# A two-group encoder layer on one core: where the weights' rounding rests and the scaled row maxima are computed

## The chip, the core and the metric

The kernel runs on one core of a Trainium2 chip. A core has a matrix engine (TensorE, in the profile PE, with its weight loads as PEld), and three engines for elementwise work: VectorE (DVE), ScalarE (ACT) and GpSimd (POOL). Each executes its own list of instructions in the order in which it stands and waits on the others by semaphores. SyncE (SP) issues the transfers (DMA) here. SBUF is the on-chip working memory, PSUM the accumulation memory into which TensorE writes. The metric is device time in microseconds (us) of one execution, as the median over runs.

## The reference

One layer is applied to two groups (prompt and sample) of 1024 tokens by 1024 channels, with the same weights:

```
h    = rms_norm(x, norm_g) * (1 + scale) + shift        # scale, shift, gate from silu(c) @ w_ada + b_ada
proj = h @ w_in                                         # 5376 columns
qa, ka, va, za, qb, kb, vb, zb, ga, gb = split(proj)
# branch A: 8 query heads, 2 key/value heads of 64, QK rms norm, axial rotary positions
oa = softmax(qa ka^T / 8) va * silu(za)
# branch B: 4 heads, two softmax maps of 64 each, 128-wide values
ob = rms_norm((softmax(q1 k1^T / 8) - lam * softmax(q2 k2^T / 8)) vb, subln_g) * (1 - lam_init) * silu(zb)
merged = sigmoid(ga) * (oa @ w_proj_a) + sigmoid(gb) * (ob @ w_proj_b)
y = x + gate * (merged @ w_out)
```

Everything is float32.

## The kernel before, in words

A float32 matrix is split in two for TensorE: a rounded part in a fast float32 format (F32R), and the rest, that is, the original minus the rounded part. A product is then three matmuls: rounded by rounded, and each rounded part by the other's rest. So every weight that is loaded passes ScalarE, which writes the rounded copy (line 179 in `split_w`, line 222 in `load_w_proj`), and a subtraction, which writes the rest (lines 181 and 223). A tile of weights (`w`) comes in four pieces, each staged in a buffer `st` by one transfer and split by one copy and one subtraction of 128x512 numbers. In `split_w` the subtraction goes to GpSimd, except that every second piece goes to VectorE while the flag `alone[0]` is set, which is the case outside the attention. In `load_w_proj` it always goes to GpSimd.

For each group the program runs through stages. The head makes keys, values and the first queries. Then come six phases of attention: phases 0 and 1 are the two halves of branch A's heads, phases 2 to 5 the heads of branch B. Beside each phase the program lays the projections that a later phase needs (`qa_gen`, `qkb_gen`, `vb_gen`, matmuls in line 514) and pieces of the gate projections (`z_gen`, line 703), so that TensorE has work while a softmax is computed elsewhere. Behind the attention come the gated outputs (`gated_gen`), the two branch projections with the merge (`merge_gen`, line 976) and the output projection (`out_gen`, line 1005).

One step of the attention, `scores`, treats 128 queries by 1024 keys. TensorE writes the scores into one of two score banks (`s`, lines 734 and 735). VectorE takes each row's negated maximum (line 736, the column `m`) and multiplies it by the row's inverse rms `rs` (line 737). ScalarE computes the exponentials with that product as bias (line 738) into a tile `p`, which frees the score bank. VectorE transposes `p` in blocks of 32 (line 771, `flip`), and in branch B combines two maps before that (line 770). Transfers (line 776) bring the blocks into place in a tile `q`. For branch A, ScalarE rounds the result (line 784, into `hi`) and VectorE subtracts (line 785), before the value matmuls (lines 796 and 797; branch B: line 836). Line 813 writes branch A's outputs `oo`. GpSimd also does the rotary positions of the projected rows (lines 546 to 556) and an inverse root (line 532) while the attention runs; their results are turned by TensorE two pieces of tokens later (`LAG`).

What sets the order: `weave` interleaves the generators of a phase by shares. Each stream has a length (for attention multiplied by `ATT_W`, for gate pieces from `Z_SHARE`) and a lead (`IN_A` for the projections, `Z_A` for the gate pieces). `fill` in the last phase runs the rest of the gate pieces and the first `16 - TAIL` pieces of branch A's merge, and `TAIL` pieces stay for the stretch behind the attention. The emitted work is then ordered on each engine by a planner that runs the program in advance, with attention steps at a higher priority. So a change of an instruction's engine changes the rows' order on all engines.

Of the kernel before, what the change touches and what calls it, by code (L numbers as in the profile page):

```python
# [12 lines left out]
F32 = mybir.dt.float32  # L13
F32R = mybir.dt.float32r
AF = mybir.ActivationFunctionType
ALU = mybir.AluOpType
# [18 lines left out]


Z_SHARE = (
    (7, 19, 5, 3, 3, 4),
    (9, 14, 7, 3, 2, 6),
)  # L40
Z_HEAD = (6, 6)
Z_HEAD_A = (-0.4, -0.45)
ATT_W = (
    (1.07, 0.837, 1.1, 0.95, 1.07, 1.52),
    (1.15, 1.354, 1.035, 1.15, 0.85, 1.069),
)
IN_A = (
    (0.1, 0.05, 0.2, 0.05, 0.15, 0.1),
    (0.1, -0.05, 0.45, 0.15, 0.15, 0.65),
)  # L50
Z_A = (
    (0.1, 0.0, 0.4, 0.0, 0.0, 0.0),
    (0.15, 0.05, 0.35, 0.15, -0.1, -0.1),
)
LAST_ATT, LAST_FILL = (44, 26)
GATED_A = -0.3
TAIL = 6
TAIL_A = 0.3
LAG = 2

# [11 lines left out]
def weave(*streams):  # L72

    live = [[g, n, 0, ahead] for g, n, ahead in streams if n > 0]
    while live:
        s = min(live, key=lambda s: s[2] / s[1] - s[3])
        if next(s[0], None) is not None:
            s[2] += 1
        else:
            live.remove(s)  # L80


def drain(*gens):
    for g in gens:
        if g is not None:
            for _ in g:
                pass
# [3 lines left out]
def kernel(ctx: ExitStack, tc: tile.TileContext, t: dict):  # L91
    nc = tc.nc
# [18 lines left out]
    def nm(s):  # L111
        uid[0] += 1
        return f"{s}_{uid[0]}"

    def sbank():
        return ps_s.tile([P, 1024], F32, tag="s", name=nm("s"))

    alone = [True]
# [57 lines left out]
    def split_w(w, q, st):  # L176
        wh = w[:, q * 2 : q * 2 + 2, 0, :]
        wl = w[:, q * 2 : q * 2 + 2, 1, :]
        nc.scalar.activation(wh, st, AF.Copy)  # L179
        e = nc.vector if alone[0] and q % 2 else nc.gpsimd  # L180
        e.tensor_tensor(out=wl, in0=st, in1=wh.bitcast(F32), op=ALU.subtract)  # L181

    def split_early(what):
        w, sts = what
        for q, st in enumerate(sts):
            split_w(w, q, st)

    def load_w(pieces, early=False):

        w = wpool.tile([P, NCH, 2, 256], F32R, tag="w", name=nm("w"))  # L190
        sts = []
        for q in range(4):
            if early:
                if q % 2 == 0:
                    room = halves2(ptile())
                st = room[q % 2].rearrange("p (c n) -> p c n", c=2)
            else:
                st = spool.tile([P, 2, 256], F32, tag="st", name=nm("st"))
            sts.append(st)
            off = 0  # L200
            for src in pieces(q):
                n = src.shape[1]
                dma(st[:, :, off : off + n], src.rearrange("(c p) n -> p c n", p=P))
                off += n
            assert off == 256
            if not early:
                split_w(w, q, st)
        return (w, sts) if early else w
# [6 lines left out]
    def load_w_proj(br, half):  # L215

        w = wpool.tile([P, 4, 2, 512], F32R, tag="w", name=nm("w"))
        mat = t["w_proj_b" if br else "w_proj_a"][0]
        for c in range(4):
            st = spool.tile([P, 512], F32, tag="st", name=nm("st"))  # L220
            dma(st, mat[c * P : (c + 1) * P, half * 512 : (half + 1) * 512])
            nc.scalar.activation(w[:, c, 0, :], st, AF.Copy)
            nc.gpsimd.tensor_tensor(out=w[:, c, 1, :], in0=st, in1=w[:, c, 0, :].bitcast(F32), op=ALU.subtract)
        return w


# [500 lines left out]
    def softmax_unit(q, rs, sw, k, pt, su):  # L727


        m = tiny.tile([P, 1], F32, tag="m", name=nm("m"))  # L730
        s = sbank()
        for n in range(2):
            sl = slice(n * 512, (n + 1) * 512)
            nc.tensor.matmul(s[:, sl], q, k[:, sl], start=True, stop=False)  # L734
            nc.tensor.matmul(s[:, sl], sw, k[:, sl], start=False, stop=True)  # L735
        nc.vector.tensor_reduce(out=m, in_=s, axis=AX.X, op=ALU.max, negate=True)  # L736
        nc.vector.tensor_tensor(out=m, in0=m, in1=rs, op=ALU.mult)  # L737
        nc.scalar.activation(  # L738
            pt.rearrange("p (j c a) -> p j c a", j=4, c=8), s.rearrange("p (c a j) -> p j c a", c=8, j=4),
            AF.Exp, scale=rs, bias=m, accum_out=su,  # L740
        )

    def scores(u, i):

        nm_ = len(u["q"])
        t, m = i // nm_, i % nm_
        qt = u["pr"] * 2 + t
        if "sw" not in u:
            u["sw"] = swapped(u)
        pt = ptile()  # L750
        su = u["su"][:, qt : qt + 1] if m == 0 else tiny.tile([P, 1], F32, tag="su", name=nm("su"))
        softmax_unit(u["q"][m][:, qt * P : (qt + 1) * P], u["rs"](qt, m), u["sw"][:, m, t * P : (t + 1) * P], u["k"][m], pt, su)
        if m == 0:
            u[t] = [pt]
        else:
            f = tiny.tile([P, 1], F32, tag="r", name=nm("r"))
            nc.vector.reciprocal(f, su)
            nc.gpsimd.tensor_scalar(
                out=f, in0=f, scalar1=u["su"][:, qt : qt + 1], scalar2=nlam, op0=ALU.mult, op1=ALU.mult
            )  # L760
            u[t] += [pt, f]
        return t if m == nm_ - 1 else None
# [190 lines left out]
    def merge_gen(st, br, oT, mT):  # L953

        for half in range(2):
            w = load_w_proj(br, half)
            for hf in range(2):
                if not br:
# [143 lines left out]
    for g in range(2):  # L1102
        st = states[g]
# [37 lines left out]
        def fill():  # L1141
# [3 lines left out]
            drain(first)  # L1145
            yield from islice(merge, 16 - TAIL)

# [3 lines left out]
        alone[0] = True  # L1151
        weave((merge, TAIL, 0.0), (then[1][0], 2, TAIL_A))
        weave((merge_gen(st, 1, oT, mT), 8, 0.0), (then[1][1], 4, 1.0))
# [58 lines left out]
```

## Time and profile before

| | us |
|---|---|
| median of 3 runs | 1973.39 (1972.16 to 1973.81) |
| span of the profiled execution, first to last instruction | 1971.9 |
| TensorE busy | 1901.8 |
| VectorE busy | 1353.0 |
| ScalarE busy | 1012.0 |
| GpSimd busy | 680.9 |

For the profiled execution only its span is shown. A row of a group of instructions gives the line, the engine, the operation, what it writes and reads, the shapes, the count (x), then the busy us, the mean ns of one, and the idle us of the engine ahead of them with what ended it ("<-"). A row of one line's instructions gives min/median/max in ns after the count. A row of waits gives the engine and line that waited, what it waited for, the us in total, the times and the longest. A row of a timeline gives start, length, engine, line and work. A row of a stretch gives its bounds and length, then PE, PEld, DVE, ACT and POOL busy with counts, the granted TensorE clock, the share of the DMA engines and GB/s. L179 is line 179 of the kernel. In the changed kernel, the lines from 180 on have the same numbers as before (only the rounded copy moves from line 179 to 180).

### The profile page before, as it was taken

To read this page: it belongs to the slowest core of one execution; us is meant where nothing else is said; L and a number is where in the kernel's file an instruction comes from. 1 tells how busy PE (TensorE), PEld (TensorE's weight loads), DVE (VectorE), ACT (ScalarE), POOL (GpSimd) and SP (SyncE) were. 2 spreads that over 40 slices of the span, in tenths; PEclk is the share of its full clock that TensorE was granted. 3 is DMA by queue.
4 is the path that set the end of the run, shared out by engine and by line. 5 is a ranking of instruction groups with operands and counts; after the bars stand their busy time and mean duration, and the time that the engine had idled before them with its cause. 6 is when DMAs were issued, how large, how long until landed. Compare 5 with 4: busy or idle time off the path is not lost. (4 is left out here: it accounts for less than half of the span.)

```text
span 1971.9 us, 30870 instructions
## 1 busy us (share of the span) xinstructions
PE 1901.8 (96%) x10466; PEld 1619.1 (82%) x10466; DVE 1353.0 (69%) x2165; ACT 1012.0 (51%) x1920; POOL 680.9 (35%) x958
## 2 busy tenths in 40 slices
PE   8999999999989999999999999999999999998999
PEld 3888888888878985778889788888888889776887
DVE  4658876786888577757465598768878766776641
ACT  4447655565655353464323576556666444447410
POOL 2363511442446251322235344114444426322210
PEclk9899999999999999999999999999999999999999
DMA  9125545556454345865641355555555334478431
GB/s 315 33 89 149 144 139 149 158 156 174 127 144 111 89 117 173 272 234 179 222 151 44 115 144 167 148 149 157 156 152 161 98 102 119 120 222 267 166 102 75
DMA packets 271614, 295.26 MB, mean 150 GB/s; under 512 B 37856, under 2 KB 220256, under 8 KB 271456
## 3 DMA queue, kind: packets, MB, share of 16 engines
q1 hardware_dynamic: 271456, 293.28, 50.1%
q8 instruction: 84, 1.38, 0.3%
q14 instruction: 74, 0.61, 0.1%
HBM read 133.72 MB, written 42.01 MB: 89 GB/s over the span
## 5 line engine op out<-in xcount | busy, mean ns | idle before, releaser
L703 PE MATMUL f<-u,w 128*128 128x512 f32 x2184 | 561.3, 395 | 3.0 <-ACT w L179 1.3
L514 PE MATMUL f<-w,u 128*128 128x256 f32 x3456 | 489.6, 286 | 5.2 <-ACT ev L709 2.7
L514 PEld LDWEIGHTS f<-w,u 128*128 128x128 f32 x3456 | 460.7, 192 | 26.8 <-ACT ev L709 3.7
L703 PEld LDWEIGHTS f<-u,w 128*128 128x128 f32 x2184 | 396.8, 189 | 78.1 <-ACT w L179 1.8
L181 POOL TENSOR_TENSOR w<-st,w 128x512 fp32r<-128x512 f32 x166 | 227.8, 1391 | 463.2 <-ACT w L179 412.9
L736 DVE TENSOR_REDUCE m<-s 128x1 f32<-128x1024 f32 x256 | 310.2, 1217 | 55.1 <-PE s L735 52.0
L771 DVE STREAM_TRANSPOSE p<-p 128x1024 f32<-128x1024 f32 x192 | 238.0, 1241 | 112.8 <-ACT p L738 110.2
L785 DVE TENSOR_TENSOR q<-q,hi 128x512 fp32r<-128x512 f32 x256 | 193.9, 774 | 47.9 <-ACT hi L784 46.4
L738 ACT ACTIVATE p<-s,m,rsB 128x1024 f32<-128x1024 f32 x128 | 154.0, 1204 | 135.0 <-DVE m L737 103.3
L738 ACT ACTIVATE p<-s,m,rsA 128x1024 f32<-128x1024 f32 x128 | 153.8, 1202 | 128.1 <-DMA q<-p 95.8
L735 PE MATMUL s<-u,sw 128*128 128x512 f32 x512 | 205.0, 401 | 0.0
L784 ACT ACTIVATE hi<-q 128x512 fp32r<-128x512 f32 x256 | 153.2, 624 | 78.2 <-DMA q<-p 50.2
L179 ACT ACTIVATE w<-st 128x512 fp32r<-128x512 f32 x196 | 114.2, 626 | 101.9 <-DMA st<-in_w_in_dram 46.6
L976 PE MATMUL f<-u,w 128*128 128x512 f32 x552 | 136.4, 400 | 11.3 <-ACT ev L709 4.1
L796 PE MATMUL a<-hi,u 128*128 128x256 f32 x512 | 132.0, 284 | 4.8 <-DVE oo L813 3.1
L976 PEld LDWEIGHTS f<-u,w 128*128 128x128 f32 x552 | 104.8, 192 | 35.3 <-DVE u L987 4.6
L836 PE MATMUL a<-q,u 128*128 128x256 f32 x512 | 125.9, 385 | 5.6 <-DMA q<-p 1.9
L797 PE MATMUL a<-q,u 128*128 128x256 f32 x512 | 129.8, 287 | 0.5 <-DVE q L785 0.4
L734 PE MATMUL s<-u 128*128 128x512 f32 x256 | 109.5, 428 | 7.9 <-ACT p L738 4.0
L734 PE MATMUL s<-u,u 128*128 128x512 f32 x256 | 103.3, 404 | 13.8 <-ACT p L738 9.0
L836 PEld LDWEIGHTS a<-q,u 128*128 128x128 f32 x512 | 95.9, 193 | 21.6 <-issue 2.9
L735 PEld LDWEIGHTS s<-u,sw 128*128 128x128 f32 x512 | 97.4, 190 | 15.5
(186 smaller groups left out, 2639.1 us busy)
## 6 DMA issues: line engine op xcount, KB each, us to landing
q<-p SPq DMA_DIRECT2D x768, 128.0 KB, 2.6
st<-in_w_in_dram SPq DMA_DIRECT2D x132, 256.0 KB, 3.0
zd<-ev SPq DMA_DIRECT2D x96, 256.0 KB, 2.2
sw<-u SPq DMA_DIRECT2D x256, 64.0 KB, 2.0
p<-zd SPq DMA_DIRECT2D x64, 256.0 KB, 3.8
u<-in_w_ada_dram SPq DMA_DIRECT2D x8, 1024.0 KB, 10.4
st<-in_w_in_dram SPq DMA_DIRECT2D x64, 128.0 KB, 2.7
st<-in_w_out_dram SPq DMA_DIRECT2D x32, 256.0 KB, 3.2
```

The costliest lines, as they stand in the source:

```text
L181: e.tensor_tensor(out=wl, in0=st, in1=wh.bitcast(F32), op=ALU.subtract)
L514: nc.tensor.matmul(ps, lt[c][:, sl], w[:, c, wi, :], start=(k == 0), stop=(k == 23))
L703: nc.tensor.matmul(ps, w[:, c, wi, e * P : (e + 1) * P], rt[c], start=(k == 0), stop=(k == 23),)
L734: nc.tensor.matmul(s[:, sl], q, k[:, sl], start=True, stop=False)
L735: nc.tensor.matmul(s[:, sl], sw, k[:, sl], start=False, stop=True)
L736: nc.vector.tensor_reduce(out=m, in_=s, axis=AX.X, op=ALU.max, negate=True)
L738: nc.scalar.activation(pt.rearrange("p (j c a) -> p j c a", j=4, c=8), s.rearrange("p (c a j) -> p j c a", c=8, j=4), AF.Exp, scale=rs, bi ...
L771: nc.vector.transpose(pt, pt)
L784: nc.scalar.activation(th, tl.bitcast(F32), AF.Copy)
L785: nc.vector.tensor_tensor(out=tl, in0=tl.bitcast(F32), in1=th.bitcast(F32), op=ALU.subtract)
L836: nc.tensor.matmul(acc, u["v"][:, k], pT[:, k], start=(k == 0), stop=(k == 7))
L976: nc.tensor.matmul(ps, w[:, c, wi, d * P : (d + 1) * P], o[:, oi, :], start=(k == 0), stop=(k == 11))
```

## The change

Three things. The subtraction that makes a weight's rest is always put on VectorE, in `split_w` and in `load_w_proj`. The product of row maximum and inverse rms in `softmax_unit` becomes an activation of ScalarE (a copy with a scale) in place of a multiplication on VectorE. And numbers that share out the phases are set anew: in `Z_SHARE`, `ATT_W`, `IN_A`, `Z_A`, and `TAIL` from 6 to 4.

```diff
 Z_SHARE = (
-    (7, 19, 5, 3, 3, 4),
-    (9, 14, 7, 3, 2, 6),
+    (6, 20, 5, 3, 3, 4),
+    (9, 14, 7, 2, 2, 7),
 )
 ATT_W = (
-    (1.07, 0.837, 1.1, 0.95, 1.07, 1.52),
+    (1.129, 0.837, 1.289, 0.95, 1.039, 1.314),
...
-TAIL = 6
+TAIL = 4
...
         nc.scalar.activation(wh, st, AF.Copy)
-        e = nc.vector if alone[0] and q % 2 else nc.gpsimd
-        e.tensor_tensor(out=wl, in0=st, in1=wh.bitcast(F32), op=ALU.subtract)
+        nc.vector.tensor_tensor(out=wl, in0=st, in1=wh.bitcast(F32), op=ALU.subtract)
...
             nc.scalar.activation(w[:, c, 0, :], st, AF.Copy)
-            nc.gpsimd.tensor_tensor(out=w[:, c, 1, :], in0=st, in1=w[:, c, 0, :].bitcast(F32), op=ALU.subtract)
+            nc.vector.tensor_tensor(out=w[:, c, 1, :], in0=st, in1=w[:, c, 0, :].bitcast(F32), op=ALU.subtract)
...
         nc.vector.tensor_reduce(out=m, in_=s, axis=AX.X, op=ALU.max, negate=True)
-        nc.vector.tensor_tensor(out=m, in0=m, in1=rs, op=ALU.mult)
+        nc.scalar.activation(m, m, AF.Copy, scale=rs)
```

Counted over the program, 168 subtractions of `split_w` and 32 of `load_w_proj` go from GpSimd to VectorE (32 of `split_w` were there already), 256 products go from VectorE to ScalarE, and ScalarE's list has 41 loads of an activation table where it had 38. All other instructions are the same in number.

In the first phase of the first group, VectorE's rows before the change (numbers behind names count the buffers; `m` is the row maximum, `s` the scores, `q` and `hi` the probabilities and their rounded part, `u` projected keys and queries):

```order
L736 TENSOR_REDUCE m_2466<-s_2467 128x1
L785 TENSOR_TENSOR q_2225<-q_2225,hi_2349 128x2x8x32
L785 TENSOR_TENSOR q_2225<-q_2225,hi_2362 128x2x8x32
L736 TENSOR_REDUCE m_2516<-s_2517 128x1
L570 TENSOR_TENSOR u_1456<-f_2733,u_1456 64x2x128
L737 TENSOR_TENSOR m_2466<-m_2466,rsA_120 128x1
L737 TENSOR_TENSOR m_2516<-m_2516,rsA_120 128x1
```

Two reductions stand together there, and the product of the first waits behind two subtractions, the second reduction and a key's subtraction. VectorE's rows of the changed kernel at the corresponding place, where the weights `w_3045` arrive (`st` is the staged piece, `ss` and `row` belong to a projected row's norm):

```order
L736 TENSOR_REDUCE m_2436<-s_2437 128x1
L181 TENSOR_TENSOR w_3045<-st_3046,w_3045 128x2x256
L181 TENSOR_TENSOR w_3045<-st_3050,w_3045 128x2x256
L181 TENSOR_TENSOR w_3045<-st_3054,w_3045 128x2x256
L570 TENSOR_TENSOR u_1456<-f_2759,u_1456 64x2x128
L530 TENSOR_REDUCE ss_2750<-row_2747 128x4
L736 TENSOR_REDUCE m_2478<-s_2479 128x1
```

The products are gone from this list, and three rests of one weight tile stand between two reductions. ScalarE's rows of the changed kernel at the same place:

```order
L180 ACTIVATE w_3045<-st_3046 128x2x256
L180 ACTIVATE w_3045<-st_3050 128x2x256
L180 ACTIVATE w_3045<-st_3054 128x2x256
L569 ACTIVATE u_1456<-f_2759 64x2x128
L528 ACTIVATE row_2747<-row_2747 128x256
L709 ACTIVATE ev_2817<-f_2612 128x512
L784 ACTIVATE hi_2261<-q_2084 128x512
L784 ACTIVATE hi_2321<-q_2180 128x512
L737 ACTIVATE m_2436<-m_2436,rsA_120 128x1
L784 ACTIVATE hi_2343<-q_2180 128x512
L738 ACTIVATE p_2435,suA_117<-s_2437,m_2436,rsA_120 128x1024
```

The rounded copies of the three pieces stand together, and the product L737 now stands in ScalarE's list behind other copies, with one more copy between it and its exponential.

More of the change, by code (lines that the diff above doesn't have):

```diff
@@ L43 @@
 ATT_W = (
-    (1.07, 0.837, 1.1, 0.95, 1.07, 1.52),
-    (1.15, 1.354, 1.035, 1.15, 0.85, 1.069),
+    (1.129, 0.837, 1.289, 0.95, 1.039, 1.314),
+    (1.255, 1.354, 1.035, 1.175, 0.85, 1.069),
 )
 IN_A = (
-    (0.1, 0.05, 0.2, 0.05, 0.15, 0.1),
-    (0.1, -0.05, 0.45, 0.15, 0.15, 0.65),
+    (0.1, 0.25, 0.2, 0.05, 0.15, 0.1),
+    (0.1, -0.05, 0.45, 0.25, 0.15, 0.65),
 )
@@ L52 @@
     (0.1, 0.0, 0.4, 0.0, 0.0, 0.0),
-    (0.15, 0.05, 0.35, 0.15, -0.1, -0.1),
+    (0.2, 0.05, 0.35, 0.35, -0.1, 0.1),
 )
-LAST_ATT, LAST_FILL = (44, 26)
+LAST_ATT = 44
+LAST_FILL = 26
 GATED_A = -0.3
-TAIL = 6
+TAIL = 4
 TAIL_A = 0.3
```

## Prediction

> **What bounds the kernel now.** I read the page's busy times first, then the list of who waited for whom, then busy times by stretch, then the lines that the change touches.
>
> ```profile
> span 1971.9 us, 30870 instructions
> PE 1901.8 (96%) x10466; PEld 1619.1 (82%) x10466; DVE 1353.0 (69%) x2165; ACT 1012.0 (51%) x1920; POOL 680.9 (35%) x958
> 1867.52 5.44 PE f L976 x24
> ```
>
> The last row (from the chain that ended last) shows PE at its undisturbed pace: 24 matmuls of 512 columns in 5.44 us, 227 ns each. The change leaves PE's work alone, so only PE's idle time can be won: 1971.9 - 1901.8 = 70.1 us, the head and the tail included. The profiled span lies 1.5 us under the median of the runs, 1973.39 us; I make the sum against the span and add the 1.5 us at the end. A move of under 0.2% (4 us) is what a measurement of this kernel cannot tell from none.
>
> Which part of the 70 us could the change reach? The list of PE's waits (time, times, longest):
>
> ```profile
> PE s L734 <- ACT p L738: 13.0, 15, 1.6
> PE s L734 <- DMA q<-p: 6.1, 4, 3.6
> PE f L976 <- ACT ev L709: 4.1, 1, 4.1
> PE f L976 <- DVE u L987: 3.9, 3, 2.6
> PE a L796 <- DVE oo L813: 3.1, 4, 1.2
> PE f L976 <- DVE row L946: 3.0, 2, 2.5
> PE a L836 <- DMA q<-p: 1.9, 3, 0.8
> PE f L703 <- POOL w L181: 0.3, 1, 0.3
> ```
>
> The largest wait is that of the next score matmuls (L734) for an exponential (L738), which frees one of two score banks: 13.0 us in 15 waits, 0.87 us each. The transfers of the transposed probabilities (6.1 + 1.9 us) and the values' output (3.1 us) hang on the same chain. That makes 24.1 us behind the softmax. For the weights' rests on POOL the PE waited 0.3 us in all.
>
> **The softmax step.** What the chain waits for, by line:
>
> ```profile
> ACT p L738 <- DVE m L737: 124.5, 59, 5.9
> L737 DVE TENSOR_TENSOR m<-m,rsA x128: 111/159/1251, 144.5 to 1467.2; 128x1 f32<-128x1 f32 x128
> L737 DVE TENSOR_TENSOR m<-m,rsA 128x1 f32<-128x1 f32 x128 | 30.1, 238 | 2.1
> L737 DVE TENSOR_TENSOR m<-m,rsB 128x1 f32<-128x1 f32 x128 | 25.9, 209 | 1.7
> L736 DVE TENSOR_REDUCE m<-s 128x1 f32<-128x1024 f32 x256 | 310.2, 1217 | 55.1 <-PE s L735 52.0
> L738 ACT ACTIVATION_READ_ACCUMULATOR p<-s,m,rsB 128x1 f32 x128 | 24.4, 191 | 0.0
> L569 ACT ACTIVATE u<-s x26: 257/274/381, 80.3 to 1093.3; 64x128 fp32r<-64x128 f32 x14, 64x256 fp32r<-64x256 f32 x12
> ```
>
> ScalarE waited 59 times for the small product L737. Its own 159 ns (the middle figure: median) is not the trouble; its place in VectorE's queue is. Where the old order puts a second reduction and two subtractions ahead of it, as in the rows of the order above, that is 1.217 + 2 x 0.686 us. The change takes 30.1 + 25.9 = 56.0 us off VectorE and gives ScalarE 256 instructions that the trace does not show. Nearest rows: 191 ns for a 128x1 read of the accumulator below, 274 ns for a small activation above. Near the lower one, since it is a 128x1, I take 0.20: 256 x 0.20 = 51 us (49 to 70) on an engine busy 1012 us. The Trainium skill's page "ScalarE: Activation LUTs" (What ACT_TABLE_LOAD costs) puts an activation with one 128x1 pointer operand at about 280 ns, by which it would be 72 us; no run yet shows which.
>
> Per softmax the chain trades 0.16 us plus its place in VectorE's queue for 0.20 us plus its place in ScalarE's. The second can also be behind other work: in the order above, one subtraction input (L784) stands between product and exponential. Bounds on the gain: at best all 24.1 us, at worst a loss as large. I take a third, -8: a wait of 0.87 us ends when a reduction of 1.217 us no longer stands in between, but only where such a pair exists and ScalarE is free.
>
> **The weights' rests.** 168 instructions of split_w and 32 of load_w_proj move from POOL to VectorE.
>
> ```profile
> L181 POOL TENSOR_TENSOR w<-st,w x166: 1259/1296/2247, 47.1 to 1926.7; 128x512 fp32r<-128x512 f32 x166
> L181 DVE TENSOR_TENSOR w<-st,w x30: 672/693/1785, 47.6 to 1931.0; 128x512 fp32r<-128x512 f32 x30
> L181 DVE TENSOR_TENSOR w<-st,w 128x512 fp32r<-128x512 f32 x30 | 31.5, 1051 | 27.4 <-ACT w L179 27.3
> L785 DVE TENSOR_TENSOR q<-q,hi x256: 631/686/1836, 159.5 to 1511.5; 128x512 fp32r<-128x512 f32 x128
> L785 DVE TENSOR_TENSOR q<-q,hi 128x512 fp32r<-128x512 f32 x256 | 193.9, 774 | 47.9 <-ACT hi L784 46.4
> 480.88 2.99 POOL L181 TENSOR_TENSOR w<-st,w 128x512 fp32r<-128x512 f32 x2
> 481.13 3.29 DVE L785 TENSOR_TENSOR q<-q,hi 128x512 fp32r<-128x512 f32 x2 [1.32 <-ACT hi L784]
> ```
>
> Cost on VectorE at the median: 200 x 0.693 = 139 us. Against it stands a relief. The last two rows are one moment: two rests run on POOL, and two subtractions beside them take 3.29 us where the median makes 1.37. So a rest on POOL stretches a two-input subtraction of VectorE by up to its own length. Over the kernel: L785 has 193.9 us against 256 x 0.686 = 175.6 at the median, 18 us too much; L181 itself 31.5 against 30 x 0.693 = 20.8, 11 us. Also L737's mean of 238 against 159, already counted in the 56. VectorE's balance: 139 - 56 - 29 = +54 us, 1353 to about 1407 us, 71% of the span. POOL loses the whole of its 228 + 44 us in these groups.
>
> ```profile
> L181 POOL TENSOR_TENSOR w<-st,w 128x512 fp32r<-128x512 f32 x166 | 227.8, 1391 | 463.2 <-ACT w L179 412.9 <-DMA od<-oo 28.4 <-DVE q L1010 18.2
> L223 POOL TENSOR_TENSOR w<-st,w 128x512 fp32r<-128x512 f32 x32 | 44.0, 1395 | 106.9 <-ACT w L222 104.7 <-DMA tab<-rA 2.2
> 150.00:770.00 620.00, 604.28 (x3544) 526.91 (x3543) 461.59 (x712) 350.82 (x681) 234.10 (x360) 0.99 0.50 139
> 1110.00:1775.00 665.00, 644.08 (x3720) 562.38 (x3719) 506.59 (x766) 375.71 (x724) 247.35 (x377) 0.99 0.52 144
> ```
>
> What hid the rests before is that POOL could sit and wait for the weight's copy on ScalarE (412.9 us) with little behind it. On VectorE the wait stands in front of reductions. The 30 rests already there waited 27.3 us, 0.91 us each. The last two rows are the two attention stretches (columns after the length: PE, PE loads, VectorE, ScalarE, POOL): PE idle 15.7 + 20.9 = 36.6 us of 1285, VectorE idle 1285 - 968.2 = 316.8. An idle us of VectorE thus went with at most 36.6 / 316.8 = 0.115 us of PE's. Bounds for the added waits: 0, if the copies are early; 168 x 0.91 = 153 us on VectorE and 17.7 on PE, if all are as late as the present ones. The planned order puts three copies ahead on ScalarE with a reduction in front of the three rests, so I take a sixth of the upper end, +3. The relief of 29 us by the same ratio is worth -3.3; the 139 us of added work fill idle time of VectorE, which the two stretches have 317 us of.
>
> The Trainium skill's page "SBUF — State Buffer" (SBUF: two separate sides) says of GpSimd and a VectorE operation with two SBUF inputs that whichever starts first holds the shared port pair and the other "fully blocks". The 3.29 us agree for VectorE as the loser. Where the rule speaks against the change: it makes 200 more holders that block POOL's rotary work, which stays there.
>
> ```profile
> L546 POOL TENSOR_TENSOR rc<-row,cosB x64: 317/323/1400, 354.8 to 1697.0; 128x64 f32<-128x64 f32 x64
> ```
>
> In rows: 323 ns at the median and 1400 at most, so a block costs POOL about 1.1 us. If one in four of the 200 met such an operation, 55 us of waits would be added to an engine that loses 272 us of work: nothing for PE, whose rotated rows are needed two pieces later (LAG).
>
> **Pieces set anew.** These move matmuls between stages and take none away. Shares of each phase shift the score matmuls among projections by a few positions; bounds are the waits of one phase either way, some 10 us (24.1 over two groups, less than half each); I take 0. TAIL 6 to 4 brings two branch-A merges of 12 matmuls forward, 2 x 12 x 0.227 = 5.4 us per group. They are cover taken from the stretch after the attention, where PE waited 4.1 + 3.9 + 3.0 us, and given to its last scores. Between -5 and +11; I take 0, since what is cover lost behind is cover won ahead. ScalarE's order holds 41 table loads instead of 38; a load is 1283 ns (median of L738's), so 3.8 us there, by the ratio 0.4 us on PE: +0.4.
>
> ```profile
> L738 ACT ACT_TABLE_LOAD  x9: 1283/1283/1283, 144.0 to 1791.5; - x9
> ```
>
> **Sum.** -8 + 3 - 3.3 + 0.4 = -7.9, so a span of 1964.0 and a time of 1965.5 us.
>
> **Rivals.** (1) Rests late on VectorE. They arrive with their weights, and while VectorE stands at one, reductions behind it let the score banks stay full. At the present mean wait of 0.91 us PE loses 17.7, against the relief of 3.3 and nothing won in the softmax: +14, 1987 us. For it: 27.3 us in front of 30 rests. Against it: those are in the stages without attention, where weights come one after another. It decides once the mean wait is over (8 + 3.3) / (168 x 0.115) = 0.58 us. (2) ScalarE's queue takes the chain's wait over: a product planned early stops the three copies L784 behind it until its reduction is done. For it: L784 feeds the value matmuls and ScalarE already waited 124.5 us at this spot. Against it: the same wait stood there before, one instruction later. If it doubles, 124.5 us more of ScalarE's idle time, of which PE's share was at most 36.6 / (1285 - 726.5) = 0.066, cost 8.2; with nothing won in the softmax, the rests' +3 and the relief of 3.3 that is +8, 1981 us. It decides once that wait passes some 245 us. (3) Nothing moves: PE has 96% and its waits are spread over many causes; what the softmax releases is met by the next wait. 1973 us. (4) More is won: the whole 24.1 us goes but for 4, with evener spacing of the scores: -20, 1953 us. It needs ScalarE always free.
>
> **Chances.** Forecast 0.50 (own range 1956 to 1969); (4) 0.12; (3) 0.14; (1) 0.14; (2) 0.10. So faster 0.62, within 0.2% 0.14, slower 0.24. The range 1950 to 1987 takes in (2) to (4) and reaches to the price of (1); what is left out is the half of (1) that comes dearer and of (4) that comes cheaper, with the unpriced tail of the pieces, about 0.2.
>
> **What will show it.** Right: the wait of L738 for L737 gone and its successor (ScalarE's L737 for the reduction) under 124.5 us; L785 near 0.69 us on average instead of 774 ns; PE's waits for L738 and the transfers at some 14 us. Wrong: VectorE's L181 waiting more than 0.58 us each on ScalarE's copy; ScalarE's L737 above 0.3 us; waits of L976 in the merges above 11 us; PE idle for more than 36.6 us in the two attention stretches.

## The result and the profile after

The changed kernel takes 1959.89 us (median of 4 runs, 1956.9 to 1963.3) against 1973.6 us before. The ratio is 0.9936, with a 95% interval from 0.9920 to 0.9952. The forecast was 1965.5 us in a range from 1950 to 1987 us: the sign is as forecast and the time lies in the range. How it came about was otherwise than forecast.

The busy times of the profiled execution after, whose time was 1959.98 us:

```profile
span 1958.3 us, 30869 instructions
PE 1896.0 (97%) x10466; PEld 1618.1 (83%) x10466; DVE 1373.1 (70%) x2109; ACT 1081.4 (55%) x2179; POOL 408.2 (21%) x758
```

PE idles 62.3 us instead of 70.1, and its busy time is 5.8 us shorter for the same 10466 matmuls. So of the 13.6 us by which the span is shorter, 7.8 are idle time and 5.8 are busy time. PE's waits after, the rows that the text speaks of:

```profile
PE s L734 <- ACT p L738: 13.2, 14, 3.5
PE f L976 <- ACT ev L709: 5.0, 1, 5.0
PE a L797 <- DVE q L785: 4.2, 3, 1.9
PE f L858 <- ACT at L851: 4.1, 1, 4.1
PE a L796 <- DVE oo L813: 4.0, 6, 1.6
PE f L514 <- ACT ev L709: 2.3, 1, 2.3
PE a L796 <- DMA q<-p: 1.4, 1, 1.4
PE f L514 <- DVE w L181: 1.1, 2, 0.6
PE f L976 <- DVE u L987: 0.6, 1, 0.6
```

The wait for the exponentials, on which the forecast's largest term rested, is unchanged: 13.2 us, before 13.0. The waits for the transposed probabilities fell from 6.1 and 1.9 us to 1.4, and the merges' waits on VectorE (L987, L946) from 6.9 to 0.6. Others grew: the value matmuls' wait for the subtraction (L797) from 0.4 to 4.2 us, and the wait at L858, not in the list before, to 4.1. The idle time that was won is a sum of small waits. In the two attention stretches PE now idles 12.6 + 17.2 = 29.8 us, before 36.6:

```profile
150.00:770.00 620.00, 607.37 (x3549) 528.58 (x3547) 475.64 (x667) 385.17 (x804) 153.04 (x301) 0.99 0.51 142
1110.00:1775.00 665.00, 647.81 (x3739) 566.71 (x3738) 518.97 (x730) 413.58 (x859) 154.97 (x307) 0.99 0.54 150
```

The 5.8 us of busy time are spread over many lines (L703 has the most, 2.0 us), and no run here tells what shortened it. By line, the instructions that the change touches:

```profile
L737 ACT ACTIVATE m<-m,rsA x128: 278/294/297, 141.1 to 1461.1; 128x1 f32<-128x1 f32 x128
ACT m L737 <- DVE m L736: 195.7, 145, 5.4
L181 DVE TENSOR_TENSOR w<-st,w x196: 645/684/1529, 47.3 to 1915.6; 128x512 fp32r<-128x512 f32 x196
DVE w L181 <- ACT w L180: 33.3, 31, 2.5
L785 DVE TENSOR_TENSOR q<-q,hi 128x512 fp32r<-128x512 f32 x256 | 172.8, 691 | 40.9 <-ACT hi L784 39.7
```

The product takes 0.294 us on ScalarE. The rests wait 33.3 us on ScalarE's copies, 0.17 us each over the 196 shown. VectorE's subtractions L785 are down from 774 ns on average to 691, close to the 686 that were their median before. Where the time went between the groups is seen from the output projection's line, first of the kernel before, then of the changed one (first and last start stand behind the durations):

```profile
L1005 PE MATMUL f<-u,w x456: 388/389/389, 932.7 to 1967.8; 128*128 128x512 f32 x152
```

```profile
L1005 PE MATMUL f<-u,w x456: 388/389/390, 925.9 to 1954.0; 128*128 128x512 f32 x152
```

The first group's output begins 6.8 us earlier, and from there to the last output matmul 1028.1 us pass instead of 1035.1. Both groups won about 7 us.

### The profile page after: what moved, and what is told of

Read it like the earlier page. It is cut to its first block, busy times and chain, and to the rows that moved or that the text cites. A ratio compares the mean times of both kernels' runs of the same rounds, so it can differ in the third digit from the quotient of the medians.

```text
span 1958.3 us, 30869 instructions
## 1 busy us (share of the span) xinstructions
PE 1896.0 (97%) x10466; PEld 1618.1 (83%) x10466; DVE 1373.1 (70%) x2109; ACT 1081.4 (55%) x2179; POOL 408.2 (21%) x758
## 4 chain that ended last, share of the span: by engine, by line
PE 69%; DVE 10%; DMA 8%; ACT 5%; issue 4%; SPq 3%; POOL 1%; ACTq 0%; DVEq 0%; POOLq 0%
PE f L703 16%; PE f L514 16%; PE f L976 5%; PE f L1005 5%; PE s L734 4%; PE a L836 4%; PE s L735 4%; PE s L1005 4%; DVE m L736 3%; DMA q<-p 3%; PE s L976 2%; PE a L797 2%; PE a L796 2%; SPq L776 2%; DVE p L771 2%
## 5 line engine op out<-in xcount | busy, mean ns | idle before, releaser
L703 PE MATMUL f<-u,w 128*128 128x512 f32 x2184 | 559.4, 395 | 0.4 <-ACT ev L709 0.3
L703 PEld LDWEIGHTS f<-u,w 128*128 128x128 f32 x2184 | 398.4, 189 | 76.9 <-ACT ev L709 0.9
L735 PE MATMUL s<-u,sw 128*128 128x512 f32 x512 | 204.9, 400 | 0.0
L785 DVE TENSOR_TENSOR q<-q,hi 128x512 fp32r<-128x512 f32 x256 | 172.8, 691 | 40.9 <-ACT hi L784 39.7
L784 ACT ACTIVATE hi<-q 128x512 fp32r<-128x512 f32 x256 | 153.7, 624 | 67.3 <-DMA q<-p 43.6
L738 ACT ACTIVATE p<-s,m,rsA 128x1024 f32<-128x1024 f32 x128 | 153.7, 1201 | 63.7 <-DMA q<-p 57.9
L738 ACT ACTIVATE p<-s,m,rsB 128x1024 f32<-128x1024 f32 x128 | 154.1, 1204 | 5.1 <-DVE p L770 1.0
L181 DVE TENSOR_TENSOR w<-st,w 128x512 fp32r<-128x512 f32 x196 | 132.5, 707 | 33.2 <-ACT w L180 32.1
L797 PE MATMUL a<-q,u 128*128 128x256 f32 x512 | 129.9, 287 | 4.2 <-DVE q L785 4.2
L836 PE MATMUL a<-q,u 128*128 128x256 f32 x512 | 125.2, 381 | 0.5 <-DMA st<-in_w_in_dram 0.4
L657 POOL TENSOR_TENSOR row<-row,gB 128x96 f32<-128x96 f32 x64 | 31.0, 484 | 452.3 <-ACT row L528 452.2
L734 PE MATMUL s<-u 128*128 128x512 f32 x256 | 109.7, 428 | 8.5 <-ACT p L738 8.4
L734 PE MATMUL s<-u,u 128*128 128x512 f32 x256 | 102.8, 402 | 7.6 <-ACT p L738 4.9
L735 PEld LDWEIGHTS s<-u,sw 128*128 128x128 f32 x512 | 97.6, 191 | 15.0
```

The costliest lines, as they stand in the source:

```text
L703: nc.tensor.matmul(ps, w[:, c, wi, e * P : (e + 1) * P], rt[c], start=(k == 0), stop=(k == 23),)
L738: nc.scalar.activation(pt.rearrange("p (j c a) -> p j c a", j=4, c=8), s.rearrange("p (c a j) -> p j c a", c=8, j=4), AF.Exp, scale=rs, bi ...
L785: nc.vector.tensor_tensor(out=tl, in0=tl.bitcast(F32), in1=th.bitcast(F32), op=ALU.subtract)
L836: nc.tensor.matmul(acc, u["v"][:, k], pT[:, k], start=(k == 0), stop=(k == 7))
```

## The experiments

The runs set three theories against each other. The softmax theory is the prediction's: the product wins by leaving VectorE's queue. The blocking theory says that the rests win by leaving GpSimd, where they held VectorE up. The numbers theory says that the new sharing of the phases wins. All times are medians; the kernel before ran beside each group of runs, at 1973.5 to 1974.5 us.

### One part at a time

The weights' rests alone:

```diff
-        e = nc.vector if alone[0] and q % 2 else nc.gpsimd
-        e.tensor_tensor(out=wl, in0=st, in1=wh.bitcast(F32), op=ALU.subtract)
+        nc.vector.tensor_tensor(out=wl, in0=st, in1=wh.bitcast(F32), op=ALU.subtract)
...
-            nc.gpsimd.tensor_tensor(out=w[:, c, 1, :], in0=st, in1=w[:, c, 0, :].bitcast(F32), op=ALU.subtract)
+            nc.vector.tensor_tensor(out=w[:, c, 1, :], in0=st, in1=w[:, c, 0, :].bitcast(F32), op=ALU.subtract)
```

> All weights' rests on VectorE, the product still on VectorE, the old numbers. Softmax theory (the prediction's: the gain comes from taking the product out of VectorE's queue): no change or a small loss, 1972 to 1978 us, L785 at about 0.69 us on average. Blocking theory (GpSimd's rests held VectorE up): most of the 13.7 us is here, 1960 to 1966 us. Numbers theory (the gain is the new sharing of the phases): within 4 us of 1973.6.

Measured: 1995.5 us, ratio 1.0098 (1.0080 to 1.0117), slower. VectorE was relieved as the blocking theory says, and it did not help. In this kernel lines stand one lower, so L784 is the subtraction that is L785 before; its row, the rests' wait, and the granted clock:

```profile
L784 DVE TENSOR_TENSOR q<-q,hi 128x512 fp32r<-128x512 f32 x256 | 173.2, 693 | 27.7 <-ACT hi L783 26.2 <-DMA zd<-ev 0.5
DVE w L180 <- ACT w L179: 36.2, 29, 3.5
core 0: 1993.7 us, clock 0.980
```

The rests wait 36.2 us in all, about as long as in the changed kernel (33.3), so the slowdown is not that VectorE stands at them. PE waits longer elsewhere, at the value matmuls of branch B (L835 here): 18.1 us in the four rows that name a transfer, against 3.2 at the same place (L836) before. The clock is 0.980 of full speed, in the kernel before 0.990; over the spans the missing shares are 39.9 us here and 19.7 us before. The blocking theory had set 1960 to 1966 us, and falls here.

The product alone:

```diff
-        nc.vector.tensor_tensor(out=m, in0=m, in1=rs, op=ALU.mult)
+        nc.scalar.activation(m, m, AF.Copy, scale=rs)
```

> The product of maximum and inverse rms on ScalarE alone, rests and numbers as before. Softmax theory: 1962 to 1968 us, PE's wait for L738 below 13 us. Blocking theory: within 4 us of 1973.6, L785 still near 0.77 us on average. Numbers theory: within 4 us of 1973.6.

Measured: 1980.77 us, ratio 1.0034 (1.0022 to 1.0046), slower, and outside what any of the theories had set. PE's longest wait and the clock:

```profile
PE s L734 <- ACT p L738: 21.3, 18, 3.7
core 0: 1977.7 us, clock 0.984
```

The wait for exponentials grew to 21.3 us. The softmax theory, as the prediction put it, falls: the product's move alone does not shorten that wait.

Both edits of engines, with the old numbers:

> Rests on VectorE and product on ScalarE, old numbers. Softmax theory and blocking theory: 1959 to 1966 us, nearly all of the gain, the numbers being worth little. Numbers theory: 1970 us or more.

Measured: 1978.4 us, ratio 1.0019 (1.0007 to 1.0032), some 4 us slower, which is the size that the forecast counts as no move. The numbers alone, with the engines as before:

> Only the new numbers, rests and product on the engines of before. Softmax and blocking theories: 1970 to 1980 us, no gain. Numbers theory: 1958 to 1966 us.

Measured: 1977.93 us, ratio 1.0008 (0.9997 to 1.0019), no difference shown. So no part wins by itself, and both engine edits together do not either; with the numbers they win 13.7 us. This left all three theories wrong as stated. A fourth came up, the fit theory: that the numbers fit the one order which the planner makes of this very program.

### One part left out

The changed kernel with the product back on VectorE (the reverse of the edit above):

> The changed kernel with the product back on VectorE; rests on VectorE and the new numbers stay. Softmax theory: loses most of the gain, 1968 to 1975 us. Blocking theory: keeps it, 1958 to 1964 us. Fit theory (the gain is that the new numbers suit the one order which the planner makes of this very program; any change of it loses them): 1968 us or more, and more in the half-speed time of the matrix engine's clock or in PE's waits of many small kinds.

Measured: 1991.73 us, ratio 1.0094 (1.0068 to 1.0120): all of the gain is lost and more. The changed kernel with the rests back on GpSimd:

> The changed kernel with the weights' rests back on GpSimd; product on ScalarE and the new numbers stay. Softmax theory: keeps the gain, 1958 to 1964 us. Blocking theory: loses it, 1968 to 1978 us, with VectorE's subtractions L785 back at some 0.76 us on average instead of 0.69. Fit theory: 1968 us or more.

Measured: 1959.79 us, ratio 0.9932 (0.9909 to 0.9956): the whole gain, without the rests' move. Against this stand the blocking theory and the fit theory, which had both set 1968 us or more. Busy times and waits with the product back, then with the rests back (in this last kernel lines stand one higher, so L735 is the score matmul that is L734 otherwise):

```profile
span 1989.1 us, 30803 instructions
PE 1904.0 (96%) x10466; PEld 1624.6 (82%) x10466; DVE 1394.6 (70%) x2365; ACT 1015.4 (51%) x1921; POOL 408.5 (21%) x758
PE s L734 <- ACT p L738: 19.4, 10, 6.1
PE a L836 <- DMA q<-p: 10.7, 6, 5.5
```

```profile
span 1955.6 us, 30904 instructions
PE 1894.4 (97%) x10466; PEld 1617.6 (83%) x10466; DVE 1308.7 (67%) x1909; ACT 1082.4 (55%) x2180; POOL 676.4 (35%) x958
PE s L735 <- ACT p L739: 11.2, 13, 2.4
```

PE idles 85.1 us with the product on VectorE and 61.2 us with it on ScalarE. The eight combinations in one table:

| rests | product | old numbers, us | new numbers, us |
|---|---|---|---|
| GpSimd | VectorE | 1973.6 (before) | 1977.93 |
| VectorE | VectorE | 1995.5 | 1991.73 |
| GpSimd | ScalarE | 1980.77 | 1959.79 |
| VectorE | ScalarE | 1978.4 | 1959.89 (changed) |

In this table the product on ScalarE and the new numbers win together, about 14 us, whichever engine makes the rests. The rests on VectorE cost 14 to 22 us while the product is there too, and next to nothing with the product on ScalarE. Each cell is one order of the program; how far an order alone moves the time comes below.

### The tail

```diff
-TAIL = 4
+TAIL = 6
```

> The changed kernel with 6 merge pieces behind the attention instead of 4. The order before the last phase stays, so this prices the tail alone. The prediction's term: within 2 us of 1959.9. Rival (the cover moved forward is worth 5.4 us per group): 1965 to 1971 us. The opposite (cover lost behind): 1950 to 1957 us.

Measured: 1962.55 us, ratio 0.9950 (0.9933 to 0.9967). That is 2.7 us above the changed kernel, over the 2 us that were set for the prediction's term, and the intervals overlap. The tail is worth little, if anything.

### Is it one lucky order?

A slight move of the numbers makes the planner lay out phase 0 and what follows anew:

```diff
-    (1.129, 0.837, 1.289, 0.95, 1.039, 1.314),
-    (1.255, 1.354, 1.035, 1.175, 0.85, 1.069),
+    (1.11, 0.837, 1.289, 0.95, 1.039, 1.314),
+    (1.235, 1.354, 1.035, 1.175, 0.85, 1.069),
```

> The changed kernel with the attention's length in phase 0 taken 1.6% shorter in both groups, engines as changed. If the gain belongs to the engines' new work, the time stays within 4 us of 1959.9. Fit theory: 1966 to 1980 us, as far off as leaving one edit out.

Measured: 1959.67 us, ratio 0.9928 (0.9900 to 0.9955), as the changed kernel, where the fit theory had set 1966 us or more. With the same nudge and the rests back on GpSimd:

> Product on ScalarE, weights' rests on GpSimd as before, new numbers with the attention's length in phase 0 taken 1.6% shorter. Product-with-numbers theory (the rests' move is worth nothing once the product is off VectorE): 1956 to 1964 us, not above the changed kernel by more than 4 us. Blocking theory: 1968 us or more. Fit theory (the earlier 1959.8 us with the rests back was a lucky order): 1966 us or more.

Measured: 1965.67 us, ratio 0.9968 (0.9953 to 0.9983), still faster than before, but 6 us above the changed kernel, more than the 4 us that were set for the theory in which the rests' move is worth nothing. And with the rests on VectorE outside the attention only:

```diff
-        nc.vector.tensor_tensor(out=wl, in0=st, in1=wh.bitcast(F32), op=ALU.subtract)
+        e = nc.vector if alone[0] else nc.gpsimd
+        e.tensor_tensor(out=wl, in0=st, in1=wh.bitcast(F32), op=ALU.subtract)
```

> The changed kernel with the weights' rests on VectorE outside the attention and on GpSimd beside it (branch projections on VectorE as changed). If rests on VectorE cost something in the attention and win something in the merges and the output projection: 1952 to 1958 us. If their place is worth nothing either way: 1956 to 1964 us.

Measured: 1968.98 us, ratio 0.9972 (0.9956 to 0.9987), above both cases that were named. With the changed kernel these are six, all with the product on ScalarE and the new numbers or numbers close to them, and each is faster than the kernel before, between 0.9928 and 0.9972, 1959.7 to 1969.0 us. The six kernels that have the product on VectorE or only old numbers take 1973.6 to 1995.5 us. PE's idle time parts them as well: 60.1 to 68.1 us against 70.1 to 85.1. So the gain is not one lucky order, but up to some 9 us of scatter come with the order and with where the rests are made. A preference for VectorE over GpSimd in the rests (-0.1 us in one pair, 6.0 us in the nudged pair) is no larger than that scatter, and neither are the losses of 4 to 7 us in the table.

One rival is left untested. The new numbers were only tried with the product on VectorE as they stand; no run looks for numbers that suit a kernel with the product there. So the runs show that this pair of edits wins, and not that the product on ScalarE would win if each kernel had numbers of its own.

### Which numbers

The changed kernel with the first group's old rows of `Z_SHARE`, `ATT_W` and `IN_A`:

> The changed kernel with the first group's old numbers in three tables (gate pieces, attention lengths, projection leads); the second group and the tail keep the new ones. If each group's numbers bring their own share of the 18.5 us between both engine edits with old numbers and with new ones: 1966 to 1972 us, the loss lying in the first group's phases 0 and 1, and the second group as fast as in the changed kernel. If only the whole set fits: 1976 us or more. If the first group's numbers do nothing: 1958 to 1962 us.

Measured: 1971.69 us, ratio 0.9994 (0.9977 to 1.0010). The changed kernel with both groups' old rows of `ATT_W` alone:

> The changed kernel with the old attention lengths in both groups, everything else as changed. If the gain of the numbers is the longer attention in phase 0 and less projection work taken early, the time is 1970 to 1980 us. If the lengths only spread the scores and leads and gate shares matter more, it stays at 1958 to 1966 us.

Measured: 1972.67 us, ratio 0.9984 (0.9967 to 1.0000). Each takes back 12 to 13 us, nearly the whole gain. The output projection's line, first with the first group's numbers old, then with the attention lengths old:

```profile
L1005 PE MATMUL f<-u,w x456: 388/389/389, 937.6 to 1969.7; 128*128 128x512 f32 x152
```

```profile
L1005 PE MATMUL f<-u,w x456: 388/389/389, 928.9 to 1967.2; 128*128 128x512 f32 x152
core 0: 1971.3 us, clock 0.984
```

Against 925.9 and 1028.1 us of the changed kernel, the first loses 11.7 us up to the first output and 4.0 us behind it; its profiled run took 1975.74 us, 4 us above the median, so the 4.0 us need not be the second group's. The second kernel loses 3.0 us up to the first output and 10.2 us behind. With the attention lengths old the clock is 0.984 in the profiled run, and over the runs half of this kernel's loss lies in the clock (next table). So the new rows of the first group are needed, taken together, and the lengths are worth some 13 us over both; that each group needs its lengths by itself was not measured, and the gate shares and the leads were not measured apart.

### The clock beside it

A span times the share that the clock lacks of full speed is the time lost to it, if PE was the bound meanwhile. Over the runs of each kernel:

| kernel | mean clock | lost, us | rest of the span, us |
|---|---|---|---|
| before (29 runs) | 0.990 | 19 | 1954 |
| rests alone | 0.981 | 37 | 1955 |
| product alone | 0.984 | 31 | 1948 |
| both, old numbers | 0.987 | 27 | 1951 |
| numbers alone | 0.989 | 21 | 1954 |
| changed | 0.988 | 23 | 1935 |
| changed, product back | 0.985 | 29 | 1960 |
| changed, rests back | 0.990 | 20 | 1938 |
| changed, first group's numbers old | 0.988 | 24 | 1947 |
| changed, attention lengths old | 0.985 | 29 | 1941 |

The gain of the change is not in the clock, which was no better. Of the 22 us that the rests alone cost, 18 are. The product alone lowers the rest of the span by 6 us and loses 12 to the clock. The traces show when the clock drops. A moment with the rests alone (behind the length: PE, PE loads, VectorE, ScalarE and GpSimd busy, then the clock):

```profile
1529.10:1532.50 3.40, 0.00 (x0) 0.00 (x0) 3.31 (x7) 1.48 (x2) 0.00 (x0) 1.00 0.77 202
1532.50:1535.90 3.40, 1.93 (x5) 1.58 (x6) 1.56 (x5) 1.63 (x4) 0.34 (x1) 0.50 0.82 211
1535.90:1539.30 3.40, 3.40 (x10) 2.64 (x9) 1.43 (x2) 0.00 (x0) 0.00 (x0) 0.50 0.33 99
```

PE idles for 3.40 us at full clock, and for the next 6.8 us the clock is half. In all 14 traces the clock is either full or half and changes in steps of 3.41 us. Between 100 us after the start and the last 4 us it fell 106 times from full to half, each time right behind a step in which PE had idled for 1.0 us or more, and no step at full clock with 2 us or more of idle time was without such a fall behind it. So most of the time lost to the clock is no cause of its own: it follows on waits of PE that fall together in one step. (The first fall, 43 to 50 us after the start in every trace, has no idle time of PE before it and is not explained by this.) The trace of the rests alone has 81 us at half clock, that of the kernel before 43.

## Why the prediction was right or wrong

The time and the sign were right, and for the size that is in part luck: the terms of the sum are not separate as the sum takes them to be, and most of them came out otherwise. By its own steps:

- **Only PE's idle time can be won.** This did not hold. The idle time fell by 7.8 us, beside a forecast of 7.9 that came from other terms, and 5.8 us more came out of PE's busy time, which the prediction had taken as fixed.
- **The softmax step, -8.** The direction held for the product's place only together with the numbers; the mechanism did not hold as put. PE's wait for the exponentials stayed (13.0 to 13.2 us) and grew with the product alone (21.3 us). The rows behind the softmax that made 24.1 us make 18.6 now (13.2 + 1.4 + 4.0), through the transfers and not through the exponentials, and the grown wait for L785 takes 3.8 of that back. Of the signs named for it, PE's waits for L738 and the transfers came as a sign of being right (14.6 us), and PE's idle time in the attention stayed under the 36.6 us that would have spoken against it (29.8). One sign of being right failed: ScalarE's wait for the reduction, 195.7 us, did not stay under 124.5. What I took for the value of a shorter chain is, in the runs, -18.1 us with the new numbers (1977.93 to 1959.79 us, rests on GpSimd) and +7.2 us with the old (1973.6 to 1980.77). The failed step is the assumption that these are separate terms.
- **The product's price, 0.20 us.** 0.294 us: 256 make 75 us, not 51, above the upper bound of 70. ScalarE's busy time, which counts overlapping instructions once, rose by 69.4 us, with the three more table loads. The row of a 128x1 accumulator read was the wrong neighbour. The Trainium skill's page "ScalarE: Activation LUTs" (What ACT_TABLE_LOAD costs), at 280 ns for one pointer operand, was close; the measured value decides.
- **The rests, +3 - 3.3.** With the product on ScalarE and the new numbers the sum of -0.3 us is near the measured 0.1 us, while the nudged pair gives 6.0 us for the rests on VectorE; the scatter of the orders is larger than the term. The relief is real (774 to 691 ns for L785) and so is the short wait (0.17 us each, under the 0.58 us at which it was to decide). VectorE's balance was sized at +54 us and came to +20: the relief reached more groups than the two that I had counted (L531 from 28.6 to 19.8 us, L983 from 26.2 to 21.9). GpSimd's rotary work was not held up more: L546 has 323 ns at the median as before, and 1185 at most.
- **Pieces set anew, 0.** Wrong: -18.5 us with both engine edits (1978.4 to 1959.89 us), and no gain without them. The bound that I set, some 10 us, was too small. `TAIL`, taken as 0, fits (2.7 us, within the intervals).
- **The first rival** (rests late on VectorE, 1987 us) has its outcome in the two kernels that keep the product on VectorE, 1995.5 and 1991.7 us, but not its mechanism: the rests waited 36.2 us there too, a fourth of the 153 us supposed.
- **The second rival**: ScalarE's wait for the reduction came to 195.7 us, above the 124.5 us before but under the 245 us from which it was to decide.

Why the product on ScalarE needs the new attention lengths is not settled. Not all of them are longer: in the first group phases 0 and 2 are, phases 4 and 5 are shorter. That the old ones lose with this product is shown; that the reason is how much projection work stands between two score steps is only a guess.

## What to carry to other kernels

Where a planner sets the order from tables of numbers, an edit of engines and the tables are one change: measure the combinations, since here each part alone lost or did nothing, and one pair won everything; numbers of its own for each assignment of engines would be the fuller comparison. Relieving an engine that is not the bound shows in its own rows and need not show in the time. With TensorE at 96% busy, a few per mille come and go with the order alone, so a nudge of a number that should not matter belongs beside every such measurement. Waits that fall close together cost twice, by themselves and by the half clock that followed them here.

## What the runs showed of the hardware that was not expected

The same matmuls met a different clock in different orders: 0.980 in the profiled run with the rests alone, 0.990 in the kernel before, where the work on TensorE is the same. The half clock followed steps of 3.41 us in which PE had idled for 1.0 us or more, and all steps with 2 us or more; it did not take a wait as long as a step. Over 29 runs of the kernel before, a lower clock went with a longer time, loosely, by some 1400 us per unit of clock; over 31 other runs of it by some 1800, beside a span of 1972 us. The small activation of 128x1 costs 0.294 us on ScalarE, where the same product took 0.159 us on VectorE.
